# A transformer block on one core: two modulation loads between the x tiles, a rounding step on ScalarE and a dot moved behind another step

## The chip, the cores and the metric

The kernel runs on one core of a Trainium2 chip. The engines are named as in the profile: PE (TensorE, matmuls), DVE (VectorE), ACT (ScalarE), POOL (GpSimd), and SP, which issues most of the DMA transfers. The metric is the time of one execution on the device, in microseconds.

## What is computed

One layer of an encoder trunk on a sequence of 1024 rows of width 1024, all in float32. The part that matters here is its beginning:

```python
c_act = jax.nn.silu(c)
mod = (c_act @ w_ada[l] + b_ada[l])[:, None, :]
sh_m, sc_m, g_m, sh_f, sc_f, g_f = jnp.split(mod, 6, axis=-1)
h = rmsnorm(x, norm_mix_w[l]) * (1 + sc_m) + sh_m
z, xbc, dt_raw, q, k, v = jnp.split(h @ w_in[l], IN_SPLITS, axis=-1)
```

After it come a state-space group and a chunked attention group, an output projection with a gated residual, a second normalised and modulated h, a gated feed-forward layer with a causal convolution, and a last normalisation.

## The kernel before

Every large product is done with operands split in two: a high part, rounded to the matrix engine's reduced format (fp32r), and a low part, the remainder. A product is then three matmuls: high by high, low by high, high by low (`mm3`, lines 75 to 78).

The opening works on the first two head pairs' columns of q, k and v (768 columns of `w_in`). h is needed with its width on the partitions, so the work goes in eight blocks (`kt` 0 to 7) of 128 of the 1024 columns of x, first for rows 0 to 511 (the first half, `hh` 0, x tiles 0 to 3), then for rows 512 to 1023 (x tiles 4 to 7). The loop is at lines 299 to 345. For a block of the first half it does this:

- `mod_col` (line 131) loads a 128 x 1024 piece of `w_ada` and takes its dot with silu(c) along the rows on DVE (line 134, shown as a CUSTOM_DVE instruction and a short read of the accumulator). This is done once for the scale and once for the shift; `mod_scale` and `mod_shift` (lines 198 to 207) make the columns `amix` and `bmix` of it, with short instructions on DVE. The scale tiles (`adat`, tag "wh") have two buffers, and so do the shift tiles (`adat2`, the two halves of one tile).
- the 128 x 768 weights are loaded to one of two `raws` buffers and split: the high part `wsh` on ACT (line 85), the low part `wsl` on DVE (line 86).
- four transposes on PE (line 323) put 512 rows of x, already divided by their root mean square, into a PSUM tile `tp`, of which there are two.
- `h_block` (line 245): ACT computes `hf` = `tp` x `amix` + `bmix` (line 246), DVE rounds it to the high part `hH` (line 247, CAST), DVE subtracts for the low part `hL` (line 248).
- PE multiplies: into four accumulators for q and k of two head pairs (lines 76 to 78) and into two tiles `vps` for v (line 58, which is the helper through which instructions in a fixed order are issued).

In the first half the last two blocks are set apart: their products for v come first (the v tail), and then those for q and k, accumulator by accumulator, each followed by `evac_qkv`, in which ACT and DVE take turns to split a finished accumulator in high and low parts (lines 82, 83, 85, 86). `T.on` (line 331) fixes the order of PE there. Line 340 copies the last accumulator aside, and the second half begins.

The normalisation of an x tile (`norm1`, line 266) is a square with a sum on ACT (line 243, `junk`), the reciprocal root on POOL in two short instructions (lines 116 and 117), and a scaling of the tile on DVE (line 271). Tiles 4 to 7 are loaded late, at blocks 3 to 6 of the first half (`XL`): a one-element copy of `amix` to the tile (line 318) holds the load back until then.

The order of the instructions on each engine is set by a scheduler, which simulates the program by its own costs. So an edit in one place can move instructions elsewhere. Transfers are issued by SP in one order; a transfer into a buffer waits there until the buffer's last reader is done, and those behind it wait too.

Of the kernel before, what the change touches and what calls it, by code (L numbers as in the profile page):

```python
# [10 lines left out]
F32 = mybir.dt.float32  # L11
F32R = mybir.dt.float32r
AF = mybir.ActivationFunctionType
ALU = mybir.AluOpType
PSUM = bass.MemoryType.PSUM

P = 128
# [20 lines left out]
SH_M, SC_M, G_M, SH_F, SC_F, G_F = (8 * i for i in range(6))  # L38


def f32(ap):
    return ap.bitcast(F32)
# [22 lines left out]
def tile_block(ctx: ExitStack, tc: tile.TileContext, x, crep, pk, w_ada, w_first, w_ft, w_z,  # L65
               w_out, w_up, w_down, bias, fnw, out, dbg=None):
    nc = tc.nc
    V, A, T = (InOrder(tc, e) for e in (nc.vector, nc.scalar, nc.tensor))
# [23 lines left out]
    wu = es_l.enter_context(tc.tile_pool(name="wu", bufs=2, reuse_waits="tile"))  # L92
# [35 lines left out]
        rawc[0] += 1  # L128
        return raws[:, rawc[0] % 2, 0:n]

    def mod_col(ft, t, at=None):
        nc.sync.dma_start(t, w_ada[ft])
        with tc.issue_after(at) if at else ExitStack():
            V.tensor_tensor_reduce(out=t, in0=t, in1=rowa, scale=1.0, scalar=0.0,
                                   op0=ALU.mult, op1=ALU.add, accum_out=modc[:, ft:ft + 1])
# [33 lines left out]
    def c4(ap):  # L169
        return ap.rearrange("p (a b) -> p a b", a=4)  # L170
# [22 lines left out]
    amix = const.tile([P, 16], F32, name="amix")[:, 0:8]  # L193
    bmix = const.tile([P, 8], F32, name="bmix")
# [22 lines left out]
    def new_pair(p):  # L217
        qk[p] = {n: [qk_tile(F32R) for _ in range(2)] for n in ("q", "kh", "kl")}
        qk[p]["v"] = vv[:, :, p % 2]
# [22 lines left out]
    def norm_to(xt, dst, ms):  # L242
        A.activation(dst, xt, AF.Square, scale=1.0 / 32.0, accum_out=ms)

    def h_block(tps, a, b, kt, hi, lo, tmp):
        A.activation(tmp, tps, AF.Identity, scale=a[:, kt:kt + 1], bias=b[:, kt:kt + 1])
        V.tensor_copy(hi, c4(tmp))
        V.tensor_tensor(lo, c4(tmp), f32(hi), ALU.subtract)

    wsh = s0.tile([P, KT, 768], F32R, name="wsh")  # L250
    wsl = yp.tile([P, 4096], F32R, tag="y", name="wsl")[:, 0:5 * 768].rearrange(
# [8 lines left out]
        xts.append(qk_tile(F32))  # L260
    for p in (0, 1):
        new_pair(p)
    for st in range(4):
        nc.sync.dma_start(xts[st], x[st * P:(st + 1) * P, :])

    def norm1(st):
        ms = stat()
# [4 lines left out]

    for st in range(4):
        norm1(st)
    adw = wu.tile([P, 2, 1024], F32, tag="w2", bufs=1, name="adat2")

    def first_qk(acc, n, hh, kts):
        w = slice(n * P, (n + 1) * P)
# [20 lines left out]
    for hh in range(2):  # L299
# [6 lines left out]
        tail = range(split_at, KT)  # L306
        for kt in range(KT):
            if hh == 0:
                mod_col(SC_M + kt, wu.tile([P, 1024], F32, tag="wh", name="adat"))
                mod_scale(amix, SC_M, NMIX, kt)  # L310
                mod_col(SH_M + kt, adw[:, kt % 2, :])
                mod_shift(bmix, SH_M, kt)
                t = raw_tile(768)
                nc.sync.dma_start(t, w_first[kt])
                split(wsh[:, kt, :], ws_lo(kt), t, A, V)
                for st in range(4, NT):
                    if XL[st - 4] == kt:
                        V.tensor_copy(xts[st][:, 0:1], amix[:, kt:kt + 1])
                        nc.sync.dma_start(xts[st], x[st * P:(st + 1) * P, :])
                        norm1(st)  # L320
            tps = tp_.pop() if tp_ else ps0.tile([P, 512], F32, tag="tp0", bufs=2, name="tp0")
            for j in range(4):
                T.transpose(tps[:, j * P:(j + 1) * P], xts[4 * hh + j][:, kt * P:(kt + 1) * P], ident)
            tmp = s0.tile([P, 512], F32, tag="hf", bufs=2, name="hf")
            hi, lo = ht(hh, kt)
            h_block(tps, amix, bmix, kt, hi, lo, tmp)
            if kt < split_at:
                for n in range(4):
                    first_qk(accs[n], n, hh, (kt,))
                first_v(vps, hh, (kt,))  # L330
# [233 lines left out]
    for ft in range(4):  # L564
        xt = bcp.tile([P, S], F32, tag="rm", bufs=2, name="xst")
        conv_mods(4 + ft, conv_silu(ft, xt, th512))
        for hh in range(2):
            tps = tp_tile()
# [262 lines left out]
    for m in range(NM):  # L831
        for n, names in (("x", ("b11",)), ("y", ("t1", "t3")), ("z", ("t2", "t4", "b21", "b22"))):
            t = gd[n, m] = dram.tile([kn(m), P, len(names), 512], F32, name=f"g{n}{m}")
# [650 lines left out]
```

## Time and profile before

| | |
|---|---|
| time, median of three runs | 1232.65 us (1231.15 to 1232.92) |
| span of the profiled execution | 1234.8 us |
| mean granted clock of PE in it | 0.984 |
| first matmul on h, first half | 19.81 us |
| DVE busy from 20 to 40 us | 20.0 of 20 us |
| PE waits at the seam of the two halves, until | 62.95 us |
| PE granted clock from 65 to 67 us | 0.50 |

A profile is of one execution, in microseconds from its first instruction. A row of a timeline has the start, the duration, the engine, the source line, the operation, the tiles written and read, and in square brackets how long the engine had been idle and what ended that. A row of the windows has a stretch, its length, the busy time and the number of instructions of PE, of its weight loads, of DVE, ACT and POOL, then the clock granted to PE as a share of full speed, the busy share of the DMA engines and GB/s. A row of the waits has who waited for what, the total, how many times, and the longest.

### The profile page before, as it was taken

Reading aid. Unit: us, or ns where it says so; the run is one execution under the profiler, and the core shown is the slowest. Engines: PE = TensorE matmul, PEld = TensorE weight load, DVE = VectorE, ACT = ScalarE, POOL = GpSimd, SP = SyncE. Lnnn points to the kernel's source line nnn. Section 1 sums busy time; section 2 is a strip of 40 time slices with the busy share of each in tenths; the row PEclk is TensorE's granted clock in tenths of the full one; section 3 lists DMA queues with packets and bytes.
Section 4 is the critical chain, followed back from the end, with each engine's and each line's share of the span. In section 5 each row is a group of like instructions: output and inputs, shape, how many; then the busy total and the mean of one; then the engine's idle time right before and its main releaser. Section 6 shows DMA issues by size and latency. Waiting matters only on the chain.

```text
span 1234.8 us, 15648 instructions
## 1 busy us (share of the span) xinstructions
PE 1169.8 (95%) x5802; PEld 983.1 (80%) x5802; DVE 944.7 (77%) x1419; ACT 589.0 (48%) x991; POOL 199.9 (16%) x174
## 2 busy tenths in 40 slices
PE   4998999989999969999999999999999999999995
PEld 3787788878878958888778888888888888888884
DVE  6836545589689667746799989888889869766976
ACT  4525555573333556666554434453434435433443
POOL 1304555575120033400000000000000000000002
PEclk9999999999999989999999999999999999999998
DMA  8712112134355301123132333222332277733533
GB/s 332 254 36 80 48 44 68 54 115 154 120 180 197 121 1 43 44 94 111 37 117 92 113 128 119 86 77 103 128 128 77 95 281 257 279 120 127 171 120 136
DMA packets 56395, 150.86 MB, mean 122 GB/s; under 512 B 5632, under 2 KB 5760, under 8 KB 54912
## 3 DMA queue, kind: packets, MB, share of 16 engines
q1 hardware_dynamic: 49264, 125.49, 29.8%
q10 hardware_dynamic: 7056, 24.38, 4.9%
q8 instruction: 45, 0.74, 0.2%
q14 instruction: 30, 0.25, 0.1%
HBM read 116.56 MB, written 29.10 MB: 118 GB/s over the span
## 4 chain that ended last, share of the span: by engine, by line
PE 80%; DVE 11%; ACT 3%; DMA 2%; issue 2%; POOL 1%; SPq 0%; DVEq 0%; POOLq 0%; ACTq 0%
PE wops L671 6%; PE dn L77 6%; PE dn L76 6%; PE dn L78 6%; PE uY L76 5%; PE uY L78 5%; PE uY L77 5%; PE uZ L78 3%; PE uZ L76 3%; PE uZ L77 3%; PE uX L76 3%; PE uX L78 3%; PE uX L77 3%; PE acc L76 2%; PE acc L77 2%; PE acc L78 2%
## 5 line engine op out<-in xcount | busy, mean ns | idle before, releaser
L903 POOL TENSOR_TENSOR st<-st,mhalf 128x1 f32<-128x1 f32 x16 | 12.7, 798 | 691.9 <-DVE st L902 680.5
L76 PE MATMUL dn<-w 128*128 128x512 f32 x308 | 111.9, 389 | 0.0
L77 PE MATMUL dn<-w 128*128 128x512 f32 x308 | 111.9, 389 | 0.0
L395 POOL TENSOR_SCALAR p<-p,st 128x640 f32<-128x640 f32 (+4 forms) x64 | 99.0, 1561 | 26.8 <-DVE st L394 23.7
L78 PE MATMUL dn<-w 128*128 128x512 f32 x308 | 103.3, 389 | 0.0
L76 PE MATMUL uY<-tH,w 128*128 128x512 f32 x256 | 99.7, 389 | 1.8 <-ACT w L58 1.8
L77 PE MATMUL uY<-tL,w 128*128 128x512 f32 x256 | 99.6, 389 | 0.0
L78 PE MATMUL uY<-tH,w 128*128 128x512 f32 x256 | 99.6, 389 | 0.0
L85 ACT ACTIVATE w<-ya 128x1024 fp32r<-128x1024 f32 (+1 forms) x41 | 39.1, 954 | 85.0 <-PE uY L78 82.7
L671 PE MATMUL wops<-hH,yhl 128*128 128x512 f32 x224 | 74.8, 402 | 3.5 <-DVE yhl L86 2.1
L76 PEld LDWEIGHTS dn<-w 128*128 128x128 f32 x308 | 57.8, 188 | 12.1
L77 PEld LDWEIGHTS dn<-w 128*128 128x128 f32 x308 | 57.8, 188 | 12.0
L78 PEld LDWEIGHTS dn<-w 128*128 128x128 f32 x308 | 57.8, 188 | 11.9
L389 DVE CUSTOM_DVE_ANT_0 p<-s,bias 128x640 f32<-128x640 f32 (+4 forms) x64 | 40.7, 650 | 26.3 <-PE tp L421 8.7
L76 PEld LDWEIGHTS uY<-tH,w 128*128 128x128 f32 x256 | 48.0, 188 | 12.0 <-ACT w L58 2.2
L78 PEld LDWEIGHTS uY<-tH,w 128*128 128x128 f32 x256 | 48.1, 188 | 10.0
L77 PEld LDWEIGHTS uY<-tL,w 128*128 128x128 f32 x256 | 48.0, 188 | 10.0
L86 DVE TENSOR_TENSOR pt<-tp,pt 128x512 fp32r<-128x512 f32 (+2 forms) x72 | 41.6, 595 | 18.4 <-ACT pt L85 11.4
L85 ACT ACTIVATE w<-xs 128x1024 fp32r<-128x1024 f32 (+1 forms) x41 | 38.9, 952 | 32.3 <-PE uY L78 32.3
L671 PEld LDWEIGHTS wops<-hH,yhl 128*128 128x128 f32 x224 | 42.4, 190 | 12.9 <-DVE yhl L86 2.5
L76 PE MATMUL s<-hH,wh 128*128 128x512 f32 x128 | 50.5, 395 | 1.5 <-DVE ct L492 1.3
L1054 DVE SCALAR_TENSOR_TENSOR a<-cv,pkt,a 128x1023 f32<-128x1023 f32 (+1 forms) x40 | 51.2, 1279 | 0.1
(444 smaller groups left out, 3428.8 us busy)
## 6 DMA issues: line engine op xcount, KB each, us to landing
gz<-a ACTq DMA_DIRECT2D x10, 1024.0 KB, 5.3
wos<-in_w_ada_dram SPq DMA_DIRECT2D x18, 512.0 KB, 4.1
ya<-in_w_up_dram SPq DMA_DIRECT2D x11, 768.0 KB, 4.1
xs<-in_w_up_dram SPq DMA_DIRECT2D x11, 768.0 KB, 4.2
adat<-in_w_ada_dram SPq DMA_DIRECT2D x16, 512.0 KB, 5.7
raws<-in_w_ft_dram SPq DMA_DIRECT2D x14, 512.0 KB, 3.5
qk<-in_w_ada_dram SPq DMA_DIRECT2D x14, 512.0 KB, 4.7
gy<-a ACTq DMA_DIRECT2D x10, 512.0 KB, 2.6
```

What stands on the lines that cost most here:

```text
L76: T.matmul(ps, lh, rh, start=start, stop=False, skip_group_check=more)
L77: T.matmul(ps, lh, rl, start=False, stop=False, skip_group_check=more)
L78: T.matmul(ps, ll, rh, start=False, stop=stop, skip_group_check=more)
L85: i = A.activation(hi, src, AF.Copy) if ehi is A else ehi.tensor_copy(hi, src)
L86: return i, elo.tensor_tensor(lo, src, f32(hi), ALU.subtract)
L389: V.tensor_tensor_reduce(out=dst, in0=src, in1=bsl, scale=-1.0, scalar=3e38, op0=ALU.add, op1=ALU.min, accum_out=nm)
L395: G.tensor_scalar(pv_, pv_, rr, None, op0=ALU.mult)
L671: i = op(*a, **k)
L903: G.tensor_tensor(r, ms, mhalf[:, 0:1], ALU.pow)
L1054: V.scalar_tensor_tensor(a[:, j:S], c[:, 0:S - j], w[2 - j], a[:, j:S], op0=ALU.mult, op1=ALU.add)
```

## The change

Three edits. First, the two modulation pieces of block 0 (one of the scale, one of the shift) are loaded between the x tiles 1 and 2, rather than after tile 3; their tiles are allocated ahead for that, and `mod_col` learns not to load again. Second, in the first half the high part of h is rounded on ACT instead of DVE; in the second half it stays on DVE. Third, the scale dot of block 1 on DVE may be issued only after the low part of h of block 0 (`issue_after`).

```diff
-    def mod_col(ft, t, at=None):
-        nc.sync.dma_start(t, w_ada[ft])
+    def mod_col(ft, t, at=None, loaded=False):
+        if not loaded:
+            nc.sync.dma_start(t, w_ada[ft])
         with tc.issue_after(at) if at else ExitStack():
...
-    def h_block(tps, a, b, kt, hi, lo, tmp):
+    def h_block(tps, a, b, kt, hi, lo, tmp, ehi):
         A.activation(tmp, tps, AF.Identity, scale=a[:, kt:kt + 1], bias=b[:, kt:kt + 1])
-        V.tensor_copy(hi, c4(tmp))
-        V.tensor_tensor(lo, c4(tmp), f32(hi), ALU.subtract)
+        if ehi is A:
+            A.activation(hi, c4(tmp), AF.Copy)
+        else:
+            V.tensor_copy(hi, c4(tmp))
+        return V.tensor_tensor(lo, c4(tmp), f32(hi), ALU.subtract).ins
...
+    adw = wu.tile([P, 2, 1024], F32, tag="w2", bufs=1, name="adat2")
+    ad0 = wu.tile([P, 1024], F32, tag="wh", name="adat"), adw[:, 0, :]
     for st in range(4):
         nc.sync.dma_start(xts[st], x[st * P:(st + 1) * P, :])
+        if st == 1:
+            nc.sync.dma_start(ad0[0], w_ada[SC_M])
+            nc.sync.dma_start(ad0[1], w_ada[SH_M])
...
-                mod_col(SC_M + kt, wu.tile([P, 1024], F32, tag="wh", name="adat"))
+                t = wu.tile([P, 1024], F32, tag="wh", name="adat") if kt else ad0[0]
+                mod_col(SC_M + kt, t, low if kt == 1 else None, loaded=kt == 0)
                 mod_scale(amix, SC_M, NMIX, kt)
-                mod_col(SH_M + kt, adw[:, kt % 2, :])
+                mod_col(SH_M + kt, adw[:, kt % 2, :], loaded=kt == 0)
...
-            h_block(tps, amix, bmix, kt, hi, lo, tmp)
+            low = h_block(tps, amix, bmix, kt, hi, lo, tmp, (A, V)[hh])
```

The scheduler makes more of it. From line 128 on the line numbers of the changed kernel are higher by 1 to 9 (134 becomes 135, 271 becomes 280). On DVE, from the low weights of block 0 to the `amix` of block 1, before (`adat` is a scale piece and `adat_166` a shift piece, each followed by its accumulator read; `st` is the sum on the way to `amix`):

```order
L86 TENSOR_TENSOR wsl<-raws,wsh 128x768
L134 ISA adat,modc<-adat,rows 128x1024
L134 ISA modc 128x1
L247 CAST hH_83<-hf 128x4x128
L134 ISA adat_166,modc<-adat_166,rows 128x1024
L134 ISA modc 128x1
L200 TENSOR_TENSOR st_72<-modc,pkt 128x1
L248 TENSOR_TENSOR hL_85<-hf,hH_83 128x4x128
L206 TENSOR_TENSOR bmix<-modc,pkt 128x1
L202 SCALAR_TENSOR_TENSOR amix<-st_72,pkt 128x1
```

Now, on DVE, the low weights of block 0 are followed by the shift dot of block 1, and then (here `adat` is the scale piece of block 1 and, the second time, of block 2; `adat_142` is the shift piece of block 2; the last row is the `amix` of block 1):

```order
L252 TENSOR_TENSOR hL_85<-hf,hH_83 128x4x128
L135 ISA adat,modc<-adat,rows 128x1024
L135 ISA modc 128x1
L207 TENSOR_TENSOR bmix<-modc,pkt 128x1
L86 TENSOR_TENSOR wsl<-raws,wsh 128x768
L135 ISA adat,modc<-adat,rows 128x1024
L135 ISA modc 128x1
L201 TENSOR_TENSOR st_72<-modc,pkt 128x1
L135 ISA adat_142,modc<-adat_142,rows 128x1024
L135 ISA modc 128x1
L201 TENSOR_TENSOR st_72<-modc,pkt 128x1
L203 SCALAR_TENSOR_TENSOR amix<-st_72,pkt 128x1
```

So the cast has left DVE, the low part of block 0 has moved ahead of block 1's scale dot, and the low weights of block 1 and both dots of block 2 have moved ahead of block 1's `amix`.

On ACT, the end of the first half before, from block 6 on (the `junk` rows are the squares of the x tiles 5, 6 and 7, the `hf` rows blocks 6 and 7, `wsh` the weights of block 7, `wh` those of a later stage):

```order
L246 ACTIVATE hf<-tp_476,bmix,amix 128x512
L243 ACTIVATE junk,st_72<-qk 128x1024
L85 ACTIVATE wsh<-raws 128x768
L246 ACTIVATE hf<-tp_496,bmix,amix 128x512
L243 ACTIVATE junk,st_72<-qk 128x1024 x2
L85 ACTIVATE wh<-raws 128x1024
L85 ACTIVATE v<-vps 128x8x64 x2
```

And now the same place on ACT, with the same tiles and `hH`, the high part:

```order
L247 ACTIVATE hf<-tp_476,bmix,amix 128x512
L249 ACTIVATE hH_83<-hf 128x4x128
L244 ACTIVATE junk,st_72<-qk 128x1024
L85 ACTIVATE wsh<-raws 128x768
L244 ACTIVATE junk,st_72<-qk 128x1024
L247 ACTIVATE hf<-tp_496,bmix,amix 128x512
L244 ACTIVATE junk,st_72<-qk 128x1024
L249 ACTIVATE hH_83<-hf 128x4x128
L85 ACTIVATE wh<-raws 128x1024 x2
```

The square of x6 has moved ahead of block 7's `hf`, and the square of x7 stands between that `hf` and its high part. On DVE the scaling of x5 and the low weights of block 7 have moved ahead of block 7's `amix`, and the scaling of x6 ahead of block 7's low part. On PE the transposes of x6 for the second half have moved ahead of block 7's part of the v tail. Of the later x tiles, SP issues x5 one transfer earlier, ahead of the scale piece of block 7. Behind the opening the order is the same but for some swaps in the first groups of the feed-forward layer's up-projection, on PE, DVE and ACT.

More of the change, by code (lines that the diff above doesn't have):

```diff
@@ L274, in tile_block @@
         norm1(st)
-    adw = wu.tile([P, 2, 1024], F32, tag="w2", bufs=1, name="adat2")
     def first_qk(acc, n, hh, kts):
```

## The prediction

> **What bounds the kernel now.** I read the page first, then the matrix engine's waits, the chain of waits from 40 to 64 us, and timelines of the opening. The page says that the matrix engine (PE) does nearly everything:
>
> ```profile
> span 1234.8 us, 15648 instructions
> PE 1169.8 (95%) x5802; PEld 983.1 (80%) x5802; DVE 944.7 (77%) x1419; ACT 589.0 (48%) x991; POOL 199.9 (16%) x174
> ```
>
> So PE is idle for 1234.8 − 1169.8 = 65 us, and only that, or matmuls that run slow, can be won. Its waits over the whole span:
>
> ```profile
> PE tp L323 <- DVE qk L271: 14.0, 4, 10.7
> PE tp L323 <- ACT hf L246: 4.7, 3, 2.7
> PE uY L76 <- ACT w L58: 1.8, 1, 1.8
> ```
>
> The first row is the start, before any x is normalised. The 2.7 us in the second is one wait, at the seam between the two sequence halves. The change touches both. The seam in the chain of waits (start, length, what):
>
> ```profile
> 49.95 1.15 ACT junk L243 x2
> 54.12 2.88 DVE qk L271
> 58.23 0.70 DVE qk L83
> 61.63 0.60 ACT k L340
> 62.95 0.66 PE tp L323 x4
> ```
>
> The chain runs from the square of x6, the last tile but one (junk, with its accumulator read), by way of POOL's reciprocal roots to the scaling of x7 on DVE, 2.88 us long, to 57.00. Only then DVE splits v (to 58.2) and q; ACT stands in order behind those splits, and its hf for the second half frees PE at 62.95. From DVE's q (58.23) to PE (62.95) is 4.72 us.
>
> Around the seam the clock matters too. Windows (stretch, its length, busy times, granted clock, DMA):
>
> ```profile
> 60.95:64.37 3.42, 1.42 (x9) 1.25 (x10) 2.13 (x5) 3.17 (x6) 0.00 (x0) 1.00 0.75 227
> 64.37:67.78 3.41, 3.41 (x14) 3.02 (x13) 3.29 (x7) 1.98 (x3) 0.00 (x0) 0.50 0.37 80
> 122.39:125.80 3.41, 2.65 (x18) 2.40 (x19) 3.32 (x9) 2.63 (x7) 3.41 (x3) 1.00 0.00 0
> 245.27:248.68 3.41, 2.28 (x16) 1.58 (x14) 3.02 (x11) 3.36 (x10) 3.09 (x3) 1.00 0.86 315
> 248.68:252.10 3.42, 3.25 (x16) 2.96 (x15) 2.32 (x7) 1.95 (x6) 3.42 (x3) 0.50 0.96 374
> ```
>
> A stretch with PE busy for 1.42 or 2.28 us of 3.41 is followed by one at clock 0.50; the next after 2.65, at 125.80, still had full clock. So somewhere between 0.8 and 1.1 us of idling in one such window costs the next window half its speed: 3.41 × 0.5 = 1.7 us. The seam costs the wait and this.
>
> **The change part by part.** *The start.* The six transfers ahead of the first weights stay six; x2 and x3 go behind the two modulation tiles, so x3 now lands last of them. The transfers' rate then (last column, GB/s), and block 0 before, by engine, with two rows from later for their durations:
>
> ```profile
> 12.00:14.00 2.00, 0.99 (x4) 0.57 (x4) 1.24 (x3) 0.78 (x2) 1.75 (x4) 1.00 1.02 412
> ```
>
> ```profile
> 15.11 0.84 ACT L85 ACTIVATE wsh<-raws 128x768 fp32r<-128x768 f32 x1 [2.34 <-DMA raws<-in_w_first_dram]
> 17.48 0.78 ACT L246 ACTIVATE hf<-tp,bmix,amix 128x512 f32<-128x512 f32 x1 [1.53 <-DVE bmix L206]
> 11.58 0.62 POOL L116 TENSOR_SCALAR st<-st 128x1 f32<-128x1 f32 x1 [0.24 <-ACT junk L243]
> 12.29 0.57 POOL L117 TENSOR_TENSOR st<-st,mhalf 128x1 f32<-128x1 f32 x1
> 12.94 0.78 POOL L116 TENSOR_SCALAR st<-st 128x1 f32<-128x1 f32 x1
> 13.80 1.39 POOL L117 TENSOR_TENSOR st<-st,mhalf 128x1 f32<-128x1 f32 x1
> 15.23 0.75 DVE L271 TENSOR_SCALAR qk<-qk,st 128x1024 f32<-128x1024 f32 x1 [0.44 <-POOL st L117]
> 17.31 0.96 DVE L86 TENSOR_TENSOR wsl<-raws,wsh 128x768 fp32r<-128x768 f32 x1
> 18.18 1.22 DVE L134 CUSTOM_DVE_ANT_0 adat<-adat,rows 128x1024 f32<-128x1024 f32 x1
> 19.33 0.42 DVE L247 CAST hH<-hf 128x512 fp32r<-128x512 f32 x1
> 16.04 0.69 PE L323 MATMUL tp<-ident,qk 128*128 128x128 f32 x2 [1.65 <-DVE qk L271]
> 19.81 2.07 PE L76 MATMUL acc<-hH,wsh 128*128 128x512 f32 x4 [0.38 <-DVE hH L247]
> 51.47 0.69 DVE L248 TENSOR_TENSOR hL<-hf,hH 128x512 fp32r<-128x512 f32 x1
> 85.72 0.62 ACT L85 ACTIVATE qk<-k 64x512 fp32r<-64x512 f32 x1
> ```
>
> ACT waited for the weights until 15.11; the 384 KB just ahead of that took about 0.95 us at the 412 GB/s of this stretch (an estimate), so x3 lands near 14.1. Its square takes 1.15 us, as x6's above (to 15.3). POOL's pair took from 11.58 to 12.86, 1.28 us, for x2 and from 12.94 to 15.19, 2.25 us, for x3, the latter under a long DVE dot. DVE will be nearly empty there, so I take 1.28: scaling at 16.6. The scaling at 15.23 let the transposes start at 16.04, and the first of the pair is what hf needs: 1.25 us from scaling to hf. So hf starts at 17.85 and ends at 18.63. The high part on ACT has no row; its nearest is the last one above, a 512-wide copy from SBUF in 0.62 us, against 0.42 on DVE. High part until 19.3, first dot at 19.35 instead of 19.81. With the 2.25 us it is 20.3. (On each engine the next instruction starts about 0.08 before the end shown for the last one: 17.31 + 0.96 against 18.18. So a cast takes 0.34 of DVE's time, low weights 0.87, a dot 1.14, a low part 0.6, a scaling 0.67.)
>
> *Block 1.* DVE's order is now: low weights, shift dot, low part of h, scale dot, low weights, both dots of block 2, and only then block 1's amix. From the scaling at 16.6: 0.67, 0.87, 1.14, then the low part 19.35 to 19.94, 1.14, 0.87, 1.14, 1.14 and some 0.2 of small ones: amix at 24.45. hf 0.78 and the high part 0.62 give block 1's dots at 26.0. Before:
>
> ```profile
> 26.09 1.17 PE L76 MATMUL acc<-hH,wsh 128*128 128x512 f32 x4
> 30.71 1.17 PE L76 MATMUL acc<-hH,wsh 128*128 128x512 f32 x4
> 46.92 0.50 PE L77 MATMUL acc<-hL,wsh 128*128 128x512 f32 x1 [0.65 <-DVE hL L248]
> 52.21 0.38 PE L58 MATMUL vps<-wsh,hL 128*128 128x256 f32 x1 [0.22 <-DVE hL L248]
> ```
>
> So the half us won at the first dot is given back one block later, and PE goes on at its own 4.6 us a block (26.09 to 30.71), bound by itself. The 20.3 above would make it 27.0, still early enough for the tail below. That the dot waits for the low part changes nothing further: PE is fed.
>
> *DVE's load.* Eight casts go, 0.34 us each: 2.7 us. The 0.65 us wait at 46.92 goes with them. What is late next is block 7's low part, which PE's v tail waits for at 52.21 before:
>
> ```profile
> 45.88 1.06 ACT L243 ACTIVATE junk<-qk 128x1024 f32<-128x1024 f32 x1 [0.80 <-DMA qk<-in_x_dram]
> 47.12 1.29 POOL L116 TENSOR_SCALAR st<-st 128x1 f32<-128x1 f32 x1 [4.12 <-ACT junk L243]
> 48.50 0.94 POOL L117 TENSOR_TENSOR st<-st,mhalf 128x1 f32<-128x1 f32 x1
> 49.00 0.15 DVE L202 SCALAR_TENSOR_TENSOR amix<-st,pkt 128x1 f32<-128x1 f32 x1
> 49.28 0.78 ACT L246 ACTIVATE hf<-tp,bmix,amix 128x512 f32<-128x512 f32 x1 [1.51 <-DVE amix L202]
> 55.86 0.58 ACT L82 ACTIVATE qk<-acc 64x512 fp32r<-64x512 f32 x1
> ```
>
> Block 7's amix stood at 49.00. Seven casts ahead of it go (−2.4); x5's scaling and block 7's low weights, behind it before, are ahead now (0.67 + 0.87 = +1.5): 48.1 with no more waiting than before. New waits come: block 5's low part stands behind x4's square on ACT (1.15), and x5's scaling behind POOL (2.35 in its rows) now ahead of the amix. I take 49.0, between 48.1 and the 51.2 of the slow rival below. From there ACT runs hf (49.3 to 50.0), then x7's square (1.15 and a gap, to 51.25), and only then the high part (to 51.9); DVE's low part follows, and 0.74 after its start PE: 52.6, 0.4 us later than 52.21. What the cast saves on DVE is lost behind a square on ACT.
>
> *The seam.* ACT's first q split started at 55.86, 3.65 us after the tail resumed: 56.25 now, and DVE's 0.6 later, 56.85. DVE itself: x6's square goes ahead of block 7's hf now, so x7's ends near 51.25, its root 1.28 later (x2's pair) at 52.55; with the scaling at 2.88 us again and the v splits (57.00 to 58.2 before), DVE is free at 56.65; with a scaling of 0.75 long before. Either way ACT's q decides, and DVE's goes from 58.23 to 56.85. By the 4.72 us of the chain above PE starts the second half at 61.6 instead of 62.95: 1.3 us sooner.
>
> *The clock.* PE's own work ended 2.7 us ahead of 62.95, at 60.25, and ends near 60.6 now: its idling at the seam shrinks from 2.7 to about 1 us, at the edge of what lost a window. But PE, which did blocks 1 to 5 at 4.6 us each from 26.0 and then six v matmuls, comes to the tail near 50 and has until 52.6 little but transposes: some 2 us idle, where the wait at 52.21 was 0.22. So I expect one lost window as before, moved from behind the seam to ahead of it, or kept: 0.
>
> *Later.* In the first up-projection groups the scheduler swaps some products and additions. The longest wait of PE there is the 1.8 us (uY) of the second view; I put 0 on the swap, between a gain and a loss of that.
>
> **The sum**: −1.3 at the seam, 0 for the clock, 0 later. Against the profiled span of 1234.8 that is 1233.5; the span lies 2.15 above the median of 1232.65 (three runs, 1231.15 to 1232.92), so the forecast is 1231.3 us. A run of this kernel can tell about 0.2%, 2.5 us, from no change.
>
> **The rivals.** *No window is lost* at either place: −1.3 − 1.7 = −3.0, 1229.6. For it: the seam's new gap of about 1 us lies between the 0.8 and the 1.1 us above, and the tail's 2 us may fall across two windows. Against it: idle shares of 1.1 us (2.28 busy) and of 2.0 (1.42 busy) each had a slow window behind them. [...]
>
> *Two windows are lost*, in the tail and at the seam: −1.3 + 1.7 = +0.4, 1233.05.
>
> *Slower: block 7's high part comes late on ACT.* If x5's tile lands no sooner (45.85), its square ends at 47.05, POOL takes 2.35 us as in its rows above, and DVE's scaling, low weights and amix end at 51.2 instead of 49.0. Then ACT's hf, x7's square and the high part end at 54.1, the tail resumes at 54.85, q goes to 59.1, 0.9 later than before, and with both windows lost it is +0.9 + 1.7 = +2.6: 1235.25. It decides from an amix of block 7 at about 51.1, where the loss passes 2.5. Against it: DVE has 2.7 us less to do, and x5 is issued one transfer earlier.
>
> That *the change does nothing at the start* is already in the forecast.
>
> **How the numbers follow.** One lost window, −1.3: 0.40. None, −3.0: 0.25. Two, +0.4: 0.18. Slower: 0.17. Faster by over 0.2% is the second and 0.05 of the first, whose lower end is near it: 0.30; slower is the last, 0.17; the rest, 0.53, within 0.2%. The likeliest alone spans 1230.4 to 1232.5 (amix at 48.1 and 50.2). Over all the range goes from 1229.0, the second case with part of the first's spread of 0.9 below it, to 1235.2, the last.
>
> **What would show it.** Right: first dot near 19.35; block 1's near 26.0; the 0.65 us wait gone; block 7's amix near 49, the tail's low part at 52.6 behind x7's square on ACT; PE at the second half near 61.6; one window at 0.50 between 50 and 68. Wrong: a tail that resumes before 51.5 or after 54, a second half that starts after 63, two slow windows or none, or a gap on PE in the up-projection.

## The result, and the profile after

The changed kernel took 1230.86 us (median of 20 runs, 1229.3 to 1233.95), the kernel before 1233.89 us (20 runs of the same sessions, 1231.15 to 1236.23). The ratio is 0.9979, 95% interval 0.9971 to 0.9988: 2.6 us faster, between 1.5 and 3.6. The forecast was 1231.3 us, 1.3 us faster. That the time itself was met within 0.5 us is in part luck: the forecast started from the 1232.65 us of three runs of the kernel before, which over 20 runs has 1233.89, and the gain was twice the one forecast; the two errors, 1.24 and 1.3 us, cancel.

The profiled execution after, its page and its longest wait of PE at the seam:

```profile
span 1230.6 us, 15650 instructions
PE 1167.7 (95%) x5802; PEld 981.7 (80%) x5802; DVE 940.0 (76%) x1411; ACT 592.7 (48%) x999; POOL 195.7 (16%) x174
```

```profile
PE tp L332 <- ACT hf L247: 2.3, 3, 1.1
```

The wait of 2.7 us at the seam of the two halves is now 1.1. The span is 4.2 us shorter, more than the median fell, so the two executions differ by something else as well. Part of it is at the very start. The square of x0 and PE's first transposes, in the timelines of before and of after:

```profile
7.74 1.06 ACT L243 ACTIVATE junk<-qk 128x1024 f32<-128x1024 f32 x1 [0.83 <-DMA qk<-in_x_dram]
10.68 0.69 PE L323 MATMUL tp<-ident,qk 128*128 128x128 f32 x2 [10.68 <-DVE qk L271]
```

```profile
6.80 1.04 ACT L244 ACTIVATE junk<-qk 128x1024 f32<-128x1024 f32 x1
9.73 0.69 PE L332 MATMUL tp<-ident,qk 128*128 128x128 f32 x2 [9.73 <-DVE qk L280]
```

In the execution of before that was profiled, ACT waited 0.83 us for the first x tile. The change doesn't touch that transfer, and another kernel with the transfers of before (the one with POOL held, below) has these transposes at 9.85. So the tile came late by chance there, and times of the opening are best counted from the first transposes. Then the timeline of after:

```profile
18.91 2.06 PE L76 MATMUL acc<-hH,wsh 128*128 128x512 f32 x4
25.64 1.19 PE L76 MATMUL acc<-hH,wsh 128*128 128x512 f32 x4
...
48.02 0.15 DVE L203 SCALAR_TENSOR_TENSOR amix<-st,pkt 128x1 f32<-128x1 f32 x1
48.95 1.05 ACT L244 ACTIVATE junk<-qk 128x1024 f32<-128x1024 f32 x1
50.51 2.08 ACT L85 ACTIVATE wh<-raws 128x1024 fp32r<-128x1024 f32 x2
50.65 0.39 PE L58 MATMUL vps<-wsh,hH 128*128 128x256 f32 x1 [0.54 <-ACT hH L249]
51.24 0.75 DVE L280 TENSOR_SCALAR qk<-qk,st 128x1024 f32<-128x1024 f32 x1
51.38 0.39 PE L58 MATMUL vps<-wsh,hL 128*128 128x256 f32 x1 [0.22 <-DVE hL L252]
51.63 4.99 POOL L86 TENSOR_TENSOR wl<-raws,wh 128x1024 fp32r<-128x1024 f32 x2 [0.60 <-ACT wh L85]
54.99 0.59 ACT L82 ACTIVATE qk<-acc 64x512 fp32r<-64x512 f32 x1 [0.79 <-PE acc L58]
55.61 0.68 DVE L83 SCALAR_TENSOR_TENSOR qk<-acc,qk 64x512 fp32r<-64x512 f32 x1 [0.69 <-ACT qk L82]
60.39 0.66 PE L332 MATMUL tp<-ident,qk 128*128 128x128 f32 x4 [1.14 <-ACT hf L247]
```

Two things are to be seen. The scaling of x7 on DVE (51.24) takes 0.75 us now, where it took 2.88, and starts ahead of POOL's two subtractions for later low weights (51.63), where it had started 0.07 behind them. POOL begins them late because it waits 0.60 us for ACT's copy `wh` (50.51), which stands behind block 7's high part on ACT. And DVE's first split of q (55.61) follows straight on ACT's (54.99 + 0.59), where it had come 1.8 us after it. The same instants, forecast and measured, as they stand and counted from the first transposes (10.68 and 9.73):

| | before | forecast | after | before, counted | forecast, counted | after, counted |
|---|---|---|---|---|---|---|
| first dot on h | 19.81 | 19.35 | 18.91 | 9.13 | 8.67 | 9.18 |
| block 1's dots | 26.09 | 26.0 | 25.64 | 15.41 | 15.32 | 15.91 |
| block 7's amix | 49.00 | 49.0 | 48.02 | 38.32 | 38.32 | 38.29 |
| tail's low part on PE | 52.21 | 52.6 | 51.38 | 41.53 | 41.92 | 41.65 |
| ACT's first split of q | 55.86 | 56.25 | 54.99 | 45.18 | 45.57 | 45.26 |
| DVE's first split of q | 58.23 | 56.85 | 55.61 | 47.55 | 46.17 | 45.88 |
| PE at the second half | 62.95 | 61.6 | 60.39 | 52.27 | 50.92 | 50.66 |

Up to ACT's split nothing is won: at block 1 the changed kernel is even half a microsecond behind, which it makes up again by block 7. All of the 1.6 us at the seam arises between ACT's split of q and DVE's. Behind the seam the spans are 1234.8 - 62.95 = 1171.85 and 1230.6 - 60.39 = 1170.21, that is 1.64 us apart, and that is one window of half clock, which before had at 64.37; their other windows of half clock behind the seam are the same ones. The windows of after around the seam, on the grid of its own clock changes (in both traces these lie 3.41 us or a whole multiple of it apart), with the columns of the windows shown before:

```profile
50.05:53.46 3.41, 2.65 (x20) 2.38 (x20) 1.72 (x3) 3.02 (x5) 2.60 (x3) 1.00 0.30 120
56.87:60.29 3.42, 2.38 (x12) 1.74 (x10) 2.07 (x3) 2.46 (x6) 0.00 (x0) 1.00 0.66 229
60.29:63.70 3.41, 3.31 (x20) 2.95 (x21) 3.19 (x6) 2.55 (x5) 0.00 (x0) 1.00 0.36 103
```

PE is idle for 0.76 us of the first and 1.04 us of the second, and neither is followed by half clock. So the 4.2 us of the two spans are 0.95 (the late tile), 1.6 (the seam) and 1.6 (the window).

### The profile page after: what moved, and what is told of

Read it like the earlier page. It is cut to its first block, busy times and chain, and to the rows that moved or that the text cites. A ratio compares the mean times of both kernels' runs of the same rounds, so it can differ in the third digit from the quotient of the medians.

```text
span 1230.6 us, 15650 instructions
## 1 busy us (share of the span) xinstructions
PE 1167.7 (95%) x5802; PEld 981.7 (80%) x5802; DVE 940.0 (76%) x1411; ACT 592.7 (48%) x999; POOL 195.7 (16%) x174
## 4 chain that ended last, share of the span: by engine, by line
PE 81%; DVE 11%; ACT 3%; issue 2%; DMA 2%; SPq 1%; POOL 0%; DVEq 0%; POOLq 0%; ACTq 0%
PE wops L680 6%; PE dn L77 6%; PE dn L76 6%; PE dn L78 6%; PE uY L76 5%; PE uY L78 5%; PE uY L77 5%; PE uZ L76 3%; PE uZ L78 3%; PE uZ L77 3%; PE uX L76 3%; PE uX L77 3%; PE uX L78 3%; PE acc L76 2%; PE acc L77 2%
## 5 line engine op out<-in xcount | busy, mean ns | idle before, releaser
L85 ACT ACTIVATE pt<-tp 128x512 fp32r<-128x512 f32 (+2 forms) x72 | 36.2, 523 | 31.1 <-PE tp L430 14.5
```

What stands on the lines that cost most here:

```text
L85: i = A.activation(hi, src, AF.Copy) if ehi is A else ehi.tensor_copy(hi, src)
```

## The experiments

All ratios are to the kernel before, run in the same session, with 95% intervals. As the clock differs from one execution to the next, a second measure is given, the *granted time*: span times mean granted clock, averaged over the executions (10 to 35 of each kernel, 6 of one). For the kernel before it was 1213.4, 1213.2 and 1213.1 us in three sessions, for the changed kernel 1212.4; its standard error is 0.1 to 0.3. The changed kernel was not run again in these three sessions, which were on three different chips (6, 1 and 5 in the record), so a comparison with it is across sessions. And granted time takes half of every microsecond at half clock as lost, also where PE would have waited anyway; clocks are recorded to 0.001, which is 1.2 us, so only averages of it mean anything.

### One edit at a time

Three kernels. The first has only the high part on ACT:

```diff
-    def h_block(tps, a, b, kt, hi, lo, tmp):
+    def h_block(tps, a, b, kt, hi, lo, tmp, ehi):
...
-        V.tensor_copy(hi, c4(tmp))
+        if ehi is A:
+            A.activation(hi, c4(tmp), AF.Copy)
+        else:
+            V.tensor_copy(hi, c4(tmp))
...
-            h_block(tps, amix, bmix, kt, hi, lo, tmp)
+            h_block(tps, amix, bmix, kt, hi, lo, tmp, (A, V)[hh])
```

> The kernel before with one edit of the three: the high part of the first half's h on ACT. Theory (the load of DVE): the changed kernel won 2.56 us at the seam of the halves because DVE, rid of eight casts, reached block 7's amix at 48.02 instead of 49.00 and x7's scaling at 51.24, ahead of POOL's low weights, so that it took 0.75 us instead of 2.88. This edit alone then gives most of it: block 7's amix at 47.8 to 48.5, the second half on PE at 60.4 to 61.2, ratio to the kernel before 0.9980 to 0.9988. Rival (the start): the gain comes from the earlier first dot on h (18.91 against 19.81), which this kernel lacks: its first dot comes at 20.0, the second half at 62.7 to 63.2, ratio 0.9997 to 1.0005.

The second has only the loads between the x tiles (the changed kernel with `V` for `(A, V)[hh]` and no `issue_after`):

> The kernel before with one edit of the three: block 0's two modulation loads between x tiles 1 and 2; the high part stays on DVE and no dot waits. Theory (the load of DVE): the first dot on h comes near 18.7, but DVE still has the eight casts, and PE's own 4.6 us a block sets the rest: block 1 not before 26.0, block 7's amix between 48.5 and 49.5, the second half at 62 to 63, ratio 0.9992 to 1.0005. Rival (the start): the 0.9 us of the first dot is kept to the seam and with it x7's scaling escapes the collision with POOL: second half at 60.5 to 61.5, ratio 0.9980 to 0.9987.

The third leaves the high part on DVE and keeps loads and wait:

```diff
-            low = h_block(tps, amix, bmix, kt, hi, lo, tmp, (A, V)[hh])
+            low = h_block(tps, amix, bmix, kt, hi, lo, tmp, V)
```

> The changed kernel without the high part on ACT: the loads between the x tiles and the dot of block 1 behind the first low part, casts on DVE. Theory (the load of DVE): no gain, as DVE does the same work as before: block 7's amix near 49, second half at 62 to 63, ratio 0.9992 to 1.0005. Rival (the start and the wait): first dot at 18.9 or a little sooner, block 1 at 25.6, second half at 60.4 to 61.2, ratio 0.9978 to 0.9986.

Measured: 0.9999 (0.9988 to 1.0011), 1.0009 (0.9998 to 1.0019) and 1.0004 (0.9994 to 1.0014); granted time 0.2 less, 0.7 more and 1.7 more than before. None of the three wins anything, so neither the theory (DVE's load) nor the rival (the start) explains the gain. The third edit alone, and the second with the third, were not run. The timelines of the high part on ACT, of the loads, and of loads and wait show what held each of them up:

```profile
51.91 2.41 POOL L86 TENSOR_TENSOR wl<-raws,wh 128x1024 fp32r<-128x1024 f32 x1 [2.49 <-ACT wh L85]
54.84 1.06 ACT L85 ACTIVATE wh<-raws 128x1024 fp32r<-128x1024 f32 x1 [1.45 <-DMA raws<-in_w_ft_dram]
55.30 0.75 DVE L274 TENSOR_SCALAR qk<-qk,st 128x1024 f32<-128x1024 f32 x1 [1.18 <-POOL st L117]
55.81 0.58 ACT L85 ACTIVATE v<-vps 128x512 fp32r<-128x512 f32 x1
61.87 0.66 PE L326 MATMUL tp<-ident,qk 128*128 128x128 f32 x4 [1.98 <-ACT hf L246]
```

```profile
51.15 2.47 POOL L86 TENSOR_TENSOR wl<-raws,wh 128x1024 fp32r<-128x1024 f32 x1 [0.53 <-ACT wh L85]
51.33 2.83 DVE L252 TENSOR_TENSOR hL<-hf,hH 128x512 fp32r<-128x512 f32 x1
54.22 0.49 PE L58 MATMUL vps<-wsh,hL 128*128 128x256 f32 x1 [2.31 <-DVE hL L252]
64.72 0.66 PE L332 MATMUL tp<-ident,qk 128*128 128x128 f32 x4 [1.14 <-ACT hf L247]
```

```profile
48.05 2.97 POOL L86 TENSOR_TENSOR wl<-raws,wh 128x1024 fp32r<-128x1024 f32 x1 [0.89 <-ACT wh L85]
48.68 3.15 DVE L86 TENSOR_TENSOR wsl<-raws,wsh 128x768 fp32r<-128x768 f32 x1
63.49 0.66 PE L332 MATMUL tp<-ident,qk 128*128 128x128 f32 x4 [1.39 <-ACT hf L247]
```

In each, the scheduler put one of POOL's subtractions (2.4 to 3.0 us) ahead of the reciprocal root of a late x tile, which POOL computes as well, and x7's scaling starts at 55.3 to 56.6, 4.1 to 5.4 us later than in the changed kernel. But that scaling takes its usual 0.75 us in all three, and it is not what makes the seam late. In the second kernel the subtraction met block 7's low part (2.83 us, where it takes 0.69 otherwise), and PE's tail waited 2.31 us for that. In the third it met block 7's low weights (3.15 us instead of 0.95), block 7's amix came at 51.75, and the tail's low part at 54.01. In the first nothing on DVE was stretched there: ACT's copy `wh` waited for its transfer until 54.84, and the split of v that DVE needs next stood behind it. So a subtraction on POOL stretched other DVE instructions that work from SBUF to SBUF as well, and where it fell came from the order.

The next experiment was put on record together with these three. Its theory is that in the kernel before, the collision of POOL's first subtraction with x7's scaling is what costs the time.

### POOL's subtractions held behind x7's scaling

The kernel before with none of the edits. A one-element instruction on POOL, whose result nobody reads, waits for the scaled tile, and the subtractions are issued behind it:

```diff
         V.tensor_scalar(xts[st], xts[st], r, None, op0=ALU.mult)
+        if st == 7:
+            held.append(G.tensor_scalar(mhalf[:, 7:8], xts[7][:, 0:1], 0.0, -0.5,
+                                        op0=ALU.mult, op1=ALU.add).ins)
...
-        split(wh, wl, t, hieng, loeng)
+        with tc.issue_after(held[0]):
+            split(wh, wl, t, hieng, loeng)
```

> The kernel before with none of the three edits: POOL's two subtractions for the low weights of a later stage (54.05, 5.21 us for both) are held behind x7's scaling by a one-element instruction on POOL that reads the scaled tile. Nothing else in the order moves. Theory (the collision is 1.8 of the 2.6 us): x7's scaling takes 0.75 instead of 2.88 us, DVE's first split of q starts when ACT's is done (56.5 instead of 58.23), PE starts the second half at 61.1 to 61.3 instead of 62.95; ratio 0.9983 to 0.9990, less where a window at half clock is saved as well. Rival (the scaling is long for another reason, or ACT's copies set the seam): the scaling stays over 2 us or the second half stays at 62.9; ratio 0.9996 to 1.0004.

Measured: 0.9981 (0.9969 to 0.9992), granted time 1.35 less. Its timeline:

```profile
53.62 0.76 DVE L273 TENSOR_SCALAR qk<-qk,st 128x1024 f32<-128x1024 f32 x1 [0.75 <-POOL st L117]
54.47 0.19 POOL L275 TENSOR_SCALAR mhalf<-qk 128x1 f32<-128x1 f32 x1 [0.88 <-DVE qk L273]
54.62 4.76 POOL L86 TENSOR_TENSOR wl<-raws,wh 128x1024 fp32r<-128x1024 f32 x2
60.71 0.66 PE L327 MATMUL tp<-ident,qk 128*128 128x128 f32 x4 [0.92 <-ACT hf L248]
```

The scaling takes 0.76, and PE starts the second half at 60.71, 50.86 after its first transposes (9.85) against 52.27 before: 1.4 us. Alone this wins as much as the three edits, as far as the intervals tell. The subtractions themselves show how the two engines met, as groups by tile (shortest, median, longest in ns, first and last start), of before and of this kernel:

```profile
L86 POOL TENSOR_TENSOR wl<-raws,wh x2: 2402/2624/2847, 54.1 to 56.4; 128x1024 fp32r<-128x1024 f32 x2
```

```profile
L86 POOL TENSOR_TENSOR wl<-raws,wh x2: 2406/2409/2412, 54.6 to 57.0; 128x1024 fp32r<-128x1024 f32 x2
```

Before, the first subtraction ran from 54.05 to 56.45 at its own pace (2.40 us, with POOL held 2.41), and the scaling, begun at 54.12, ended at 57.00, 0.55 after it; the second subtraction took 2.85 instead of 2.41. So the scaling seems not to have run slower beside POOL, but to have stood still until the first subtraction was over, and the second to have waited for the scaling. The stretched low part and low weights above end 0.54 and 0.81 us after their subtraction, again a little less than they take alone. The splits of q and v on DVE, which read PSUM, took their 0.6 to 0.7 us beside the same subtractions (with POOL held 1.28 for two of v from 54.29 and 0.68 for one of q from 55.98). The standing still is read from starts and ends alone; what makes one engine wait for the other, no row shows.

### The scaling of x7 moved into the subtractions

The changed kernel, with the scaling written behind the first low part of v:

```diff
+        if st == 7:
+            return r
         V.tensor_scalar(xts[st], xts[st], r, None, op0=ALU.mult)
...
-            split(o[:, :, 0, :], o[:, :, 1, :], ...)
+            i = split(o[:, :, 0, :], o[:, :, 1, :], ...)
+            if hh == 0 and b == 0:
+                with tc.issue_after(i[1].ins):
+                    V.tensor_scalar(xts[7], xts[7], r7, None, op0=ALU.mult)
...
-                        norm1(st)
+                        r7 = norm1(st)
```

> The changed kernel, with one instruction moved: x7's scaling on DVE is held behind the first of the two low parts of v, so that it falls into POOL's two subtractions (51.63 to 56.62) again. Theory (the collision carries most of the gain): the scaling takes 2.5 to 2.9 us instead of 0.75, the second low part of v starts near 56.5 instead of 54.23 and DVE's first split of q near 57.2 instead of 55.61; PE starts the second half 1.4 to 1.9 us later than in the changed kernel, at 61.8 to 62.3; ratio to the kernel before 0.9990 to 1.0003. Rival (the gain is DVE's and ACT's lighter load, the place of the scaling does not matter): the second half starts within 0.4 us of 60.39, ratio 0.9975 to 0.9984.

Measured: 0.9988 (0.9977 to 0.9999), granted time 1.0 less than before, as the changed kernel's 0.8 to 1.0. The timeline and the subtractions:

```profile
53.69 0.75 DVE L310 TENSOR_SCALAR qk<-qk,st 128x1024 f32<-128x1024 f32 x1
60.24 0.66 PE L337 MATMUL tp<-ident,qk 128*128 128x128 f32 x4 [1.14 <-ACT hf L247]
```

```profile
L86 POOL TENSOR_TENSOR wl<-raws,wh x2: 2412/2630/2849, 51.5 to 53.8; 128x1024 fp32r<-128x1024 f32 x2
```

The experiment missed its aim. The first subtraction ended at 51.48 + 2.41 = 53.89, only 0.2 us after the scaling's start, and this time the second one took 2.85 instead of 2.41. So it says nothing of what a full collision costs the kernel, only that a scaling at the seam of two subtractions pays none. The scaling ended 0.55 us after the first subtraction, as in the kernel before, though it had begun 0.20 and not 2.33 us ahead of that end; but at its 0.75 us it ends there unhindered as well, so this does not settle how the two engines met.

### Without the wait

The changed kernel without its third edit:

```diff
-                mod_col(SC_M + kt, t, low if kt == 1 else None, loaded=kt == 0)
+                mod_col(SC_M + kt, t, loaded=kt == 0)
```

> The changed kernel without its third edit: the loads between the x tiles and the high part on ACT, but block 1's scale dot is free to go ahead of the first low part. The order puts block 7's hf ahead of x6's square again, so x7's square comes one square later. Theory (what counts is that x7's scaling on DVE comes before POOL's subtraction starts, or early enough): x7's scaling starts at 52.5 or later, meets the subtraction and takes 2.5 to 2.9 us, PE starts the second half at 61.5 to 62.3, ratio to the kernel before 0.9988 to 1.0002. Rival (the two edits that lighten DVE and the start are the gain, the wait is idle): second half at 60.2 to 60.8, ratio 0.9976 to 0.9985.

Measured: 1.0014 (1.0006 to 1.0023), slower than before; granted time 1.2 more.

```profile
53.59 5.23 POOL L86 TENSOR_TENSOR wl<-raws,wh 128x1024 fp32r<-128x1024 f32 x2
53.65 2.90 DVE L280 TENSOR_SCALAR qk<-qk,st 128x1024 f32<-128x1024 f32 x1 [0.75 <-POOL st L117]
62.97 0.66 PE L332 MATMUL tp<-ident,qk 128*128 128x128 f32 x4 [2.58 <-ACT hf L247]
```

The collision is back, 0.06 us after POOL's start, and so is the wait of 2.6 us. The third edit concerns block 1, at 18 us; without it the order at 50 us is another one. There x6's square stands behind block 7's `hf` on ACT again, so x7's square comes at 51.42 instead of 48.95, and x7's scaling just behind POOL's start. No window of half clock follows the seam there, though PE waited 2.58 us: the first product by `wsl` behind it, at 65.42, took 0.40 us, where that of the kernel before, in its window of half clock at 66.21, took 0.63.

### Block 7's high part on DVE, with and without the collision

The tail waits for the high part, which stands behind x7's square on ACT. In the changed kernel, block 7's cast goes back to DVE:

```diff
-            low = h_block(tps, amix, bmix, kt, hi, lo, tmp, (A, V)[hh])
+            low = h_block(tps, amix, bmix, kt, hi, lo, tmp, A if hh == 0 and kt < 7 else V)
```

> The changed kernel with the high part of block 7 alone back on DVE, where it no longer stands behind x7's square on ACT. My reading of the tail (the high part waits for that square): hf still ends near 49.05, the high part follows by 49.5 instead of 50.6, the tail's first low-part matmul comes near 50.8 instead of 51.38 and everything to the seam moves by 0.4 to 0.7 us: second half at 59.7 to 60.0, ratio to the kernel before 0.9970 to 0.9977. Rival (the tail waits for x6's transposes or for POOL, the high part is not what is late): second half within 0.2 us of 60.39, ratio 0.9976 to 0.9983.

Measured: 0.9990 (0.9980 to 1.0000), granted time 1.5 less than before. The ratio lies above both ranges. The tail resumed at 50.59 instead of 51.38, and most of that was lost on the way:

```profile
49.75 1.04 ACT L85 ACTIVATE wh<-raws 128x1024 fp32r<-128x1024 f32 x1
51.21 5.22 POOL L86 TENSOR_TENSOR wl<-raws,wh 128x1024 fp32r<-128x1024 f32 x2
51.28 2.89 DVE L280 TENSOR_SCALAR qk<-qk,st 128x1024 f32<-128x1024 f32 x1 [0.75 <-POOL st L117]
60.12 0.66 PE L332 MATMUL tp<-ident,qk 128*128 128x128 f32 x4 [1.65 <-ACT hf L247]
```

This also shows what let the changed kernel escape. With block 7's high part off ACT, the copy `wh` runs at 49.75, POOL no longer waits for it and begins its subtraction right behind x7's root, 0.07 us ahead of the scaling. So in the changed kernel it was the second edit, by its place in ACT's order, that kept POOL back.

The same kernel with POOL held, as above, and no other instruction moved:

> The kernel with block 7's high part on DVE (the run before it of that name), and POOL's two subtractions held behind x7's scaling; nothing else moves against that kernel. There x7's scaling took 2.89 us from 51.28 and PE started the second half at 60.12, although its tail had resumed 0.64 us sooner than the changed kernel's. Theory (the collision ate the tail's gain): the scaling takes 0.75, DVE's first split of q follows ACT's at 54.8 instead of 55.40, PE starts the second half at 59.4 to 59.7, ratio to the kernel before 0.9968 to 0.9981. Rival (ACT's copies set the seam): second half at 60.0 to 60.2, ratio as there, 0.9985 to 0.9995.

Measured: 0.9984 (0.9975 to 0.9993), granted time 1.55 less.

```profile
51.07 0.75 DVE L282 TENSOR_SCALAR qk<-qk,st 128x1024 f32<-128x1024 f32 x1 [0.75 <-POOL st L117]
59.39 0.66 PE L336 MATMUL tp<-ident,qk 128*128 128x128 f32 x4 [1.14 <-ACT hf L249]
```

In the trace the seam is 0.73 us sooner, and the scaling takes 0.75, as the theory had it. The ratio just misses both ranges, and the granted times of the two kernels differ by 0.05 us only; with standard errors of 0.2 each that does not confirm the 0.7 us over all executions.

### The clock at the seam

Idle time of PE at the seam is filled with matmuls whose result is overwritten, in the changed kernel (nine of 256 columns) and in the kernel before (seven of 512):

```diff
+            if hh == 1 and kt == 0:
+                with tc.issue_after(tail_end):
+                    for i in range(9):
+                        T.matmul(vps[0][:, 0], hth[0][:, 0, 0, :], wsh[:, 0, 512:768],
+                                 start=True, stop=True)
             if kt < split_at:
...
             A.activation(k1, accs[3], AF.Copy)
+            tail_end = T.last
```

> The changed kernel with nine more matmuls of 256 columns (about 1.05 us, into a PSUM tile that is overwritten afterwards) in PE's gap of 1.14 us at the seam; nothing else in the order moves, and what they compute is not used. Theory (a gap of about 1.1 us costs a window at half clock in some executions and not in others): the second half starts where it did, the mean granted clock of the executions rises from 0.9860 to 0.9863 to 0.9873, and the time falls by 0.3 to 1.5 us: ratio to the kernel before 0.9967 to 0.9977. Rival (the clock at the seam is already full in the changed kernel): clock and time as in the changed kernel, ratio 0.9977 to 0.9983.

> The kernel before with seven more matmuls of 512 columns (about 1.6 us, not used afterwards) in PE's gap of 2.66 us at the seam, which leaves some 1.0 us idle there. Theory (the gap of the kernel before costs a window at half clock, 1.7 us, in nearly every execution, one of 1.0 us in some): the second half starts no sooner than before, the mean granted clock rises from 0.9849 to 0.9855 to 0.9863, and the time falls by 0.7 to 1.7 us: ratio 0.9986 to 0.9994. Rival (what follows the seam is not bound by PE's clock): the clock rises and the time does not, ratio 0.9997 to 1.0005.

Measured: 0.9994 (0.9983 to 1.0004) with a mean clock of 0.9860, and 1.0005 (0.9995 to 1.0015) with 0.9858; the kernel before had 0.9858 in that session. The seam of the filled changed kernel and that of the filled kernel before:

```profile
58.76 1.31 PE L339 MATMUL vps<-wsh,hH 128*128 128x256 f32 x9
59.92 0.99 PE L332 MATMUL tp<-ident,qk 128*128 128x128 f32 x5
```

```profile
60.31 1.86 PE L330 MATMUL vps<-wsh,hH 128*128 128x512 f32 x7
63.17 0.66 PE L323 MATMUL tp<-ident,qk 128*128 128x128 f32 x4 [0.78 <-ACT hf L246]
```

The gaps are filled, to nothing and to 0.8 us, and neither clock nor time improves. For the changed kernel the clock is as the rival had it, so its gap seems to cost none; the ratio lies outside the ranges of both. For the kernel before, my theory that the gap costs a window in nearly every execution isn't borne out. The kernel without the wait speaks against it too: its seam had nearly the same wait, 2.58 us, and no window of half clock behind it. But the mean clock of the kernel before moved from 0.9849 to 0.9858 between two sessions, on two chips, with nothing changed in it, which is 1.1 us, so a window in a part of the executions can't be excluded.

### The second half's first block ahead of the tail

At the seam PE waits for `hf`, which ACT makes only behind four splits and a copy. The second half's first block is written ahead of the tail (in the loop it is then left out), in the kernel with POOL held and block 7 on DVE:

```diff
+        if hh == 0:
+            tps1 = ps0.tile([P, 512], F32, tag="tp0", bufs=2, name="tp0")
+            for j in range(4):
+                T.transpose(tps1[:, j * P:(j + 1) * P], xts[4 + j][:, 0:P], ident)
+            tmp = s0.tile([P, 512], F32, tag="hf", bufs=2, name="hf")
+            h_block(tps1, amix, bmix, 0, *ht(1, 0), tmp, V)
         T.on, T.last = True, None
```

> The last kernel, and the second half's first block (its transposes, hf and parts) written ahead of the first half's tail, so that ACT makes its hf behind the first split of q instead of behind all four and the copy. Theory (at the seam PE only waits because ACT's hf stands behind splits that PE does not need): PE's gap at the seam, 1.65 us with block 7 on DVE, falls below 0.5 us, no window there is at half clock, and the second half's first matmuls follow the tail at 58.6 to 59.2; ratio to the kernel before 0.9955 to 0.9972. Rival (the accumulators, not hf, hold PE up, so the gap only moves behind the first matmuls): second half's accumulating matmuls start no sooner than 60, ratio 0.9970 to 0.9985.

The same in the kernel before, with POOL held and none of the three edits:

> The kernel before with none of the three edits, with POOL's subtractions held behind x7's scaling and the second half's first block written ahead of the tail. Theory (the seam is all there is to gain in the opening): the same gap is closed from here, the second half's first matmuls come about 2.3 to 3.3 us sooner than in the kernel before (62.95), ratio 0.9962 to 0.9980, near that of the kernel which has the three edits as well. Rival (the edits bring something of their own besides the seam): at least 0.0010 behind that kernel.

Measured: 0.9967 (0.9954 to 0.9980) and 0.9973 (0.9963 to 0.9983), granted time 3.2 and 2.8 less than before. The first one's timeline at the seam:

```profile
55.03 0.78 ACT L249 ACTIVATE hf<-tp,bmix,amix 128x512 f32<-128x512 f32 x1 [0.20 <-PE tp L348]
58.27 0.71 PE L337 MATMUL tp<-ident,qk 128*128 128x128 f32 x5
59.29 0.40 PE L76 MATMUL acc<-hH,wsh 128*128 128x512 f32 x1
```

ACT makes `hf` behind the first split (55.03, where the changed kernel has 59.56), and PE goes from the tail (to 58.27) into the second half with no gap. By granted time both beat the changed kernel (1212.4, from other sessions) by 2.0 to 2.5 us, with 1209.9 and 1210.4; the intervals of the ratios overlap its 0.9971 to 0.9988. They don't differ from each other by more than can be told, and the second has none of the three edits. So the seam is where the gain was, and what the edits bring besides is too small to be seen here: 0.5 us, with a standard error of 0.4.

## Why the prediction was right, point by point

- **Where the gain lies** was right: at the seam, between ACT's first split of q and DVE's, because the scaling of x7 no longer holds DVE up. Counted from the first transposes the seam was forecast at 50.92 and measured at 50.66. The holding of POOL in the kernel before shows the cause: with nothing else moved the seam comes 1.4 us sooner. But the prediction took the 2.88 us as they stood and gave no reason for them; that POOL causes them, and how the changed order escapes them, it did not foresee.
- **That either price of the scaling would do** was half of that step. With 0.75 us, measured, DVE was ready long before ACT. The kernel without the wait shows that 2.9 us does not always do: it must also start early. The prediction had x7's root done at 52.55 and a scaling of 2.88 end at 55.4; in that kernel it began at 53.65 and DVE came 1.3 us late to q (57.77, ACT's split ending at 56.5).
- **The start**: the forecast won 0.46 us at the first dot. Counted from the first transposes it won nothing (9.13 to 9.18), and block 1 came 0.5 later. The apparent 0.9 us is the late first tile of the execution that was profiled. That it didn't matter for the end was right: the tail came within 0.12 of before's. (The 0.08 us by which the next instruction starts ahead of the end shown is not to be seen on each engine: for DVE it is 18.18 against 18.27, but POOL's started at 12.29, behind an end at 12.20. The forecast used it for DVE alone.)
- **Block 7** went as forecast: amix 38.32 and 38.29; the high part behind x7's square on ACT (48.95, then 50.0), with PE's wait of 0.54 for it. The tail's low part was forecast 0.39 later than before and came 0.12 later.
- **The clock** is where the sum failed. I expected some 2 us of idling ahead of the tail and one window lost. PE idled 0.54 + 0.22 us there, as transposes and the matmuls of v kept it busy until 50.1, and no window around the tail and the seam is at half clock. That is the first rival, which had a chance of 0.25 and 1229.6 us. Two of the prediction's own signs of being wrong came with it: no slow window between 50 and 68, and a tail that resumed before 51.5, at 51.38, though the second is the late first tile. The limit of 0.8 to 1.1 us of idling, on which this step rested, doesn't hold in the trace it was read from: before, the windows at 456.89 and 617.32 had PE busy for 1.98 and 1.63 of 3.41 us, and the clock behind both was 1.00. In the profiled pair this window is 1.64 us. Over all executions 2.6 us were measured, of which the seam accounts for 1.6 in the trace and 0.8 to 1.0 in granted time. The rest is clock and its scatter; the fillers did not tie it to the seam, and how much of it is steady stays open.
- **Later**: 0 was right. The swaps in the up-projection cost nothing, as behind the seam the spans differ by one window alone.
- **The slow rival** didn't come: block 7's amix was at 48.02, far from 51.1. An amix that late, 51.75, came in the kernel with loads and wait, and the kernel without the wait was slower than before; both by a collision with POOL, which the prediction did not have.

## What to carry to other kernels

When a kernel's order comes from a scheduler, an edit is worth what the order makes of it: here three edits, of which none of the parts that were run wins anything, came out well together because one DVE instruction at 51 us fell ahead of a POOL instruction instead of just behind it. Look for a DVE instruction that takes a multiple of its usual time in the chain (here 2.88 us for 0.75), see what POOL began just before it (here 0.07 us), and hold that back; one short instruction did as much as the whole change. Test a rule for the clock on all windows of a trace, and not only on those that were followed by half clock. Before comparing two profiles stage by stage, find the first event that chance has shifted, and count from there.

## What the runs showed of the hardware

- The scaling of x7 on DVE from SBUF to SBUF (128 x 1024 float32) took 0.75 us (0.75 or 0.76 with POOL held), and 2.88 to 2.90 us where it began 0.06 or 0.07 us after a 2.4 us subtraction on POOL: in the kernel before, in the same with the gap filled, without the wait, and with block 7 on DVE. In the kernel before it ended 0.55 us after that subtraction, and the next subtraction took 2.85 us, 0.45 longer.
- It was not the scaling alone: a subtraction on DVE with operands in SBUF was stretched from 0.69 to 2.83 us (the kernel with the loads; begun 0.18 us after one on POOL) and one from 0.95 to 3.15 us (with loads and wait; 0.63 us after). DVE's splits that read PSUM kept their 0.6 to 0.7 us.
- The busy time of PE in a window of 3.41 us didn't by itself tell whether half clock follows: before, it followed 1.42 and 2.28 us, and not 1.63 and 1.98; after the seam waits of 1.98 us (high part on ACT) and 2.58 us (without the wait), with 1.50 and 1.70 us busy, it didn't follow either. What decides stays open.
- The first x tile, whose transfer comes first in all 14 profiled kernels, came late in two of the executions: ACT waited 0.83 and 1.71 us for it and began its square at 7.74 us (the kernel before) and 8.51 (the same with the gap filled), in the others between 6.67 and 7.01.
